# Turning the FFN's activations with transposing DMAs of 16-bit halves, and keeping the tokens stationary in ten of eleven input projections

## The chip, the cores and the metric

The kernel runs on one core of a Trainium2 chip. The metric is device time in microseconds for one execution; the time before is the median of three runs. Engines are named as the profile names them: PE multiplies matrices (PEld is its weight loader, which works beside it), DVE does elementwise vector work, ACT evaluates functions and copies, POOL is the general-purpose engine, and SP issues the DMAs. SBUF is the memory next to the engines (128 partitions); the banks of PSUM receive what PE computes. "Stationary" is the operand that is loaded into PE, "moving" the one that streams through it.

## The reference, cut to what matters

A trunk of two layers over 256 tokens of width 1024, in float32. Each layer is a half-step FFN, a mixer (attention and an mLSTM side by side), and a second half-step FFN, so the kernel computes four FFNs:

```
h = rmsnorm(x, g_pre)                      # 256 x 1024
gate, up = split(h @ w_in, 2)              # w_in: 1024 x 5632
y = (silu(gate) * up) @ w_out              # w_out: 2816 x 1024
x = x + 0.5 * rmsnorm(y, g_post)
```

## The kernel before, in words

**Tiling.** The 256 tokens are two tiles of 128 (`t` = 0, 1). The hidden width of 2816 is cut into eleven chunks of 256 columns, numbered 0 to 10. A chunk needs three weight pieces of 1 MB each: two halves of the input projection (512 rows of `w_in` each, with the chunk's 256 gate and 256 up columns), and one of the output projection (256 rows of `w_out`). The pieces are laid out in DRAM in the order of use, and SP loads them one after another into three buffers (`wr`).

**Float32 from three products.** Each operand is split into a high part in the matmul's 32-bit format and the rest: ACT writes the high part (`wh`, `hh`; line 287 for weights, 545 for activations), DVE the rest (`wl`, `hl`; 288 and 546). A product is high·high + high·rest + rest·high. Weights are split by half pieces (128 x 1024). The split halves live in 7 `wh` and 7 `wl` buffers, and three in ten of them in a further pool of six (`k4`), so about ten halves are held at a time; a `wr` buffer is free for the next load when both its halves have been split.

**Two forms of the input projection.** In chunks 0 and 1 (`TURN = 2`) the tokens are stationary: 128 x 128 blocks of the normalised input are loaded, and 512 weight columns (256 gate, 256 up) stream past. Per chunk that is 2 token tiles x 8 blocks of the width x 3 products = 48 matmuls of 512 columns (`in_piece`, lines 400 to 402). The result has tokens on partitions; ACT takes silu of the gate (line 265, called from 525), DVE multiplies (529), and PE then has to transpose it, 128 x 128 at a time (line 536, four per chunk), because the output projection needs the hidden index on partitions. In chunks 2 to 10 the weights are stationary (`in_turned`): per chunk 4 blocks of 128 hidden columns x 8 blocks of the width, each once with 512 moving columns (both token tiles, high and rest, line 611) and once with 256 (the rest of the weights against the high tokens, line 616), 32 + 32 matmuls. The result comes out already turned, in four banks; ACT and DVE add the two halves of the 512 columns, scale by the token's norm, which now lies along the free dimension (`rows`, made by two PE transposes on line 556), and apply silu and the product (lines 567, 568, 569, 265, 572, two blocks per chunk).

**The output projection** (`out_part`, lines 400 to 402) takes 24 matmuls of 512 columns per chunk, with the turned activations stationary, into four banks that accumulate over the whole FFN. Work is written so that the output projection of a chunk comes after the input projection of the chunk two later (`DEFER = 3`); in the last chunk (10) the remaining three follow.

**What sets the order.** A scheduler orders each engine's instructions when the program is built; every engine then runs its own list strictly in order, and waits at an instruction until its inputs are there. SP's list holds nearly all DMAs, so a DMA that waits there holds those behind it. Only the first chunk of all and the end of each FFN have an order of PE that is written out by hand.

Of the kernel before, what the change touches and what calls it, by code (L numbers as in the profile page):

```python
# [18 lines left out]
F32R = mybir.dt.float32r  # L19
AF = mybir.ActivationFunctionType  # L20
ALU = mybir.AluOpType
# [3 lines left out]
P = 128  # L25
D = 1024
S = 256
NT = S // P
L = 2
DFF = 2816  # L30
NC_FF = DFF // 256
# [5 lines left out]
TURN = 2  # L37
# [93 lines left out]
class _Trunk:  # L131
# [16 lines left out]
    for _n in ("nat", "ra", "rb", "rv", "tmp", "y", "so", "xg"):  # L148
        TAGS[_n] = ("ev", 5)
# [374 lines left out]
    def ffn_hidden(self, pin, r):  # L524
        nc = self.nc
        sil = self.t2("sil", (P, 256))
        self.func(sil, pin[:, 0:256], AF.Silu, scale=r)
        h = self.t2("h", (P, 256))
        nc.vector.scalar_tensor_tensor(h, pin[:, 256:512], r, sil, op0=ALU.mult, op1=ALU.mult)
        return h  # L530

    def ffn_split(self, h):
        nc = self.nc
        ptr = self.bank_tr((P, 2, P))
        for k in range(2):
            nc.tensor.transpose(ptr[:, k, :], h[:, k * P:(k + 1) * P], self.ident)
        hh, hl = self.ffn_operand()
        self.ffn_hilo(ptr, hh, hl)
        return [(hh[:, k, :], hl[:, k, :]) for k in range(2)]
# [7 lines left out]

    def ffn_evac(self, pin, r):
        return self.ffn_split(self.ffn_hidden(pin, r))
# [25 lines left out]
    def ffn_turned(self, banks, rows, late):  # L575


        ops = [self.ffn_operand() for _ in range(2)]
        for j in range(2):
            h = self.ffn_block(banks[j], rows)  # L580
            if late:
                for t in range(NT):
                    self.ffn_hilo(h[:, t], *(v[:, j] for v in ops[t]))
            else:
                self.ffn_hilo(h, *ops[j])
        return [[tuple(v[:, j] for v in ops[t]) if late else tuple(v[:, t] for v in ops[j]) for j in range(2)] for t in range(NT)]

    def ffn(self, pre, gi_post):
# [14 lines left out]
        def in_turned(banks, w, both, last):  # L603


            blocks = [(banks[j][i], slice(i * 256 + j * P, i * 256 + j * P + P)) for j in range(2) for i in range(2)]
            for group, khs in ((blocks, (0,)), (blocks[:2], (1,)), (blocks[2:], (1,))) if last else ((blocks, (0, 1)),):
                for kh in khs:
                    for b, c in group:
                        for k in range(4):  # L610
                            self.nc.tensor.matmul(b, self.cols(w[kh], k)[0][:, c], both[kh][:, k].rearrange("p i t -> p (i t)"),  # L611
                                                  start=kh == 0 and k == 0, stop=False, skip_group_check=True)
                for b, c in group:
                    for kh in khs:
                        for k in range(4):
                            self.nc.tensor.matmul(b[:, 0:NT * P], self.cols(w[kh], k)[1][:, c], both[kh][:, k, 0:NT].rearrange("p i t -> p (i t)"),  # L616
                                                  start=False, stop=kh == 1 and k == 3, skip_group_check=True)

        po, pend = None, []
        if not xT:  # L620
# [12 lines left out]
            h = [self.ffn_evac(pins[t], r[t]) for t in range(NT)]  # L633
            begin = 1
        else:
# [6 lines left out]
            ha = self.ffn_hidden(pa, r[0])  # L642
            yield "second"
            in_piece(0, 0, pa1, w1[0])
            ha = self.ffn_split(ha)
# [6 lines left out]
            hb = self.ffn_evac(pb, r[1])  # L652
            pend = [(0, [ha, hb], self.piece())]
            pb1 = self.bank_pin()
            ha1 = self.ffn_evac(pa1, r[0])
            in_piece(1, 0, pb1, w1[0])
            in_piece(1, 1, pb1, w1[1])
            po = [[self.bank_bk() for _ in range(2)] for _ in range(NT)]
            for t in range(NT):
                out_part(0, t, *pend[0][1:])  # L660
            pend = []
            h = [ha1, self.ffn_evac(pb1, r[1])]
            begin = 2
        for c in range(begin, NC_FF):
# [5 lines left out]
            if c < TURN:  # L670
                pins = [self.bank_pin() for _ in range(NT)]
                for kh in range(2):
                    for t in range(NT):
                        in_piece(t, kh, pins[t], ws[kh])
                h = [self.ffn_evac(pins[t], r[t]) for t in range(NT)]
            else:
                if c == TURN:
                    rows, both = self.token_scales(r), list(self.both)
                banks = [[self.bank_pin() for _ in range(2)], [self.bank_tr() for _ in range(2)]]
                in_turned(banks, ws, both, c == NC_FF - 1)  # L680
                if c == NC_FF - 1:
                    break
                h = self.ffn_turned(banks, rows, c > NC_FF - DEFER - 1)
            if len(pend) == DEFER - 1 or po is None:
                if po is None:
                    po = [[self.bank_bk() for _ in range(2)] for _ in range(NT)]
                cc, hc, wo = pend.pop(0)
                for t in range(NT):
                    out_part(cc, t, hc, wo)

        yield "ending"
        pend.append((c, self.ffn_turned(banks, rows, True), self.piece()))
# [564 lines left out]
```

## Time and profile before

| | |
|---|---|
| median of 3 runs | 974.04 us (973.89 to 974.1) |
| span of the profiled execution | 972.0 us |
| PE busy | 964.9 us, 99% of the span |
| PEld, DVE, ACT busy | 84%, 71%, 58% |
| DMA: bytes, mean rate | 178.94 MB, 184 GB/s |

The profiled execution is shown by its span, from the first to the last instruction; the runs' times also hold what lies around it, some 2 us. Shares are averages over stages of different kinds, so the stage of the FFN that is changed has to be read by itself: a timeline gives the start of every instruction in us from the span's start, how long the group lasts, and, in brackets, how long the engine sat idle before it and for whom. A PE group "x16" is sixteen matmuls in a row, and since they overlap, the cost of one is the distance of starts and not the duration that is listed.

### The profile page before, as it was taken

The numbers are of one execution on the slowest core, as the hardware profiler recorded it, in microseconds if no ns is written. First come the engines' busy times: TensorE is split into PE (matmuls) and PEld (weight loads), VectorE is DVE, ScalarE is ACT, GpSimd is POOL, SyncE is SP. The second block draws the span as 40 slices with busy tenths as digits, with TensorE's granted clock in tenths as the row PEclk, the third lists the DMA queues.
The fourth block names the chain that finished last, engine by engine and source line by source line (L and its number), as shares of the span: only waits on it lengthen the run. The fifth ranks groups of instructions, "written<-read, shape, count | busy, mean of one in ns | idle before, by whom it ended". The sixth has DMA issues, their size and how long they took to land.

```text
span 972.0 us, 13466 instructions
## 1 busy us (share of the span) xinstructions
PE 964.9 (99%) x5067; PEld 818.6 (84%) x5067; DVE 693.2 (71%) x1177; ACT 564.4 (58%) x1041; POOL 30.1 (3%) x55
## 2 busy tenths in 40 slices
PE   9999999999999999999999999999999999999997
PEld 6888888888888888888888888888888888888886
DVE  6786667689867676757687676776998686576764
ACT  7655555577856555555475555455778475645542
POOL 2000000000020000000000000000001000000000
PEclk9999999999999999999999999999999999999999
DMA  8954545336342844554455454543454255555421
GB/s 313 344 185 173 198 187 217 130 130 238 119 185 97 315 168 179 184 206 169 178 212 211 163 214 176 200 190 122 172 205 173 88 206 218 204 182 209 158 102 44
DMA packets 27648, 178.94 MB, mean 184 GB/s; under 512 B 3034, under 2 KB 4186, under 8 KB 6846
## 3 DMA queue, kind: packets, MB, share of 16 engines
q1 hardware_dynamic: 27006, 177.46, 49.5%
q8 instruction: 40, 0.66, 0.3%
q10 hardware_dynamic: 576, 0.61, 0.2%
q14 instruction: 26, 0.21, 0.1%
HBM read 177.01 MB, written 1.05 MB: 183 GB/s over the span
## 4 chain that ended last, share of the span: by engine, by line
PE 99%; DMA 0%; DVE 0%; SPq 0%; ACT 0%; POOLq 0%; issue 0%; DVEq 0%; ACTq 0%
PE pin L611 13%; PE ptr L611 13%; PE bk L400 10%; PE bk L401 10%; PE bk L402 10%; PE pin L400 7%; PE pin L402 7%; PE pin L401 7%; PE ptr L616 7%; PE pin L616 7%; PE ptr L879 1%; PE ptr L426 1%; PE bk L1094 1%; PE bk L1132 1%; DMA x<-in_x_dram 0%; PE bk L378 0%
## 5 line engine op out<-in xcount | busy, mean ns | idle before, releaser
L288 DVE TENSOR_TENSOR wl<-wr,wh 128x1024 fp32r<-128x1024 f32 x324 | 386.0, 1221 | 95.9 <-ACT wh L287 44.8
L287 ACT ACTIVATE wh<-wr 128x1024 fp32r<-128x1024 f32 x324 | 329.1, 1052 | 140.4 <-PE bk L402 38.6
L611 PE MATMUL pin<-both,wh 128*128 128x512 f32 x576 | 142.8, 391 | 0.0
L611 PE MATMUL ptr<-both,wh 128*128 128x512 f32 x576 | 141.5, 390 | 0.0
L400 PE MATMUL bk<-wh,hh 128*128 128x512 f32 x352 | 137.7, 391 | 0.0
L401 PE MATMUL bk<-wl,hh 128*128 128x512 f32 x352 | 137.4, 390 | 0.0
L402 PE MATMUL bk<-wh,hl 128*128 128x512 f32 x352 | 136.2, 389 | 0.0
L611 PEld LDWEIGHTS ptr<-both,wh 128*128 128x128 f32 x576 | 107.3, 188 | 21.9
L611 PEld LDWEIGHTS pin<-both,wh 128*128 128x128 f32 x576 | 107.0, 188 | 21.5
L400 PE MATMUL pin<-wh,both 128*128 128x512 f32 x304 | 122.4, 404 | 0.0
L401 PE MATMUL pin<-wl,both 128*128 128x512 f32 x304 | 119.1, 392 | 0.0
L402 PE MATMUL pin<-wh,both 128*128 128x512 f32 x304 | 118.9, 391 | 0.0
L568 DVE TENSOR_TENSOR su<-pin,su 128x256 f32<-128x256 f32 x72 | 29.3, 421 | 88.1 <-ACT su L567 87.6
L616 PEld LDWEIGHTS pin<-both,wl 128*128 128x128 f32 x576 | 76.0, 191 | 4.1
L402 PEld LDWEIGHTS bk<-wh,hl 128*128 128x128 f32 x352 | 66.1, 188 | 13.9
L616 PE MATMUL pin<-both,wl 128*128 128x256 f32 x576 | 77.7, 283 | 0.0
L545 ACT ACTIVATE hh<-su 128x256 fp32r<-128x256 f32 (+1 forms) x96 | 32.3, 358 | 77.2 <-DVE su L572 47.2
L400 PEld LDWEIGHTS bk<-wh,hh 128*128 128x128 f32 x352 | 66.2, 188 | 12.6
L401 PEld LDWEIGHTS bk<-wl,hh 128*128 128x128 f32 x352 | 66.3, 188 | 12.1
L616 PE MATMUL ptr<-both,wl 128*128 128x256 f32 x576 | 75.8, 283 | 0.0
L616 PEld LDWEIGHTS ptr<-both,wl 128*128 128x128 f32 x576 | 73.1, 192 | 1.3
L402 PEld LDWEIGHTS pin<-wh,both 128*128 128x128 f32 x304 | 57.1, 188 | 12.4
(202 smaller groups left out, 999.8 us busy)
## 6 DMA issues: line engine op xcount, KB each, us to landing
wr<-in_w_dram SPq DMA_DIRECT2D x162, 1024.0 KB, 4.9
gpost<-in_gpost_dram SPq DMA_DIRECT2D x6, 512.0 KB, 5.7
wr<-in_w_dram SPq DMA_DIRECT2D x2, 512.0 KB, 6.4
wr<-in_w_dram SPq DMA_DIRECT2D x3, 256.0 KB, 4.6
x<-in_x_dram SPq DMA_DIRECT2D x3, 256.0 KB, 5.2
out_dram<-x SPq DMA_DIRECT2D x2, 256.0 KB, 2.3
x<-in_x_dram SPq DMA_DIRECT2D x2, 128.0 KB, 2.8
wr<-in_w_dram ACTq DMA_DIRECT2D x1, 256.0 KB, 3.2
```

Source lines behind the costliest of these rows:

```text
L287: ia = nc.scalar.activation(hi, raw[:, j], AF.Copy)
L288: iv = nc.vector.tensor_tensor(lo, raw[:, j], hi.bitcast(F32), op=ALU.subtract)
L400: mm(ps, xh, wh, start=start, stop=False)
L401: mm(ps, xh, wl, start=False, stop=False)
L402: mm(ps, xl, wh, start=False, stop=stop)
L426: nc.tensor.transpose(ptr[:, k, :], x[:, (4 * hf + k) * P:(4 * hf + k + 1) * P], self.ident)
L545: self.nc.scalar.activation(hh, h, AF.Copy)
L568: nc.vector.tensor_tensor(su[:, i], bank[i][:, 0:n], su[:, i], op=ALU.add)
L611: self.nc.tensor.matmul(b, self.cols(w[kh], k)[0][:, c], both[kh][:, k].rearrange("p i t -> p (i t)"), start=kh == 0 and k == 0, stop=Fals ...
L616: self.nc.tensor.matmul(b[:, 0:NT * P], self.cols(w[kh], k)[1][:, c], both[kh][:, k, 0:NT].rearrange("p i t -> p (i t)"), start=False, sto ...
L879: self.T(ptr[:, b, :], a[:, b * P:(b + 1) * P], self.tr.ident)
L1094: self.mm(pcs[c][:, h, :], self.qkT[0][rows, h0 + h, t * P:(t + 1) * P], self.qkT[1][rows, h0 + h, 0:nk], start=True, stop=True)
```

## The change

`TURN` goes from 2 to 10: chunks 0 to 9 now keep the tokens stationary, and only chunk 10 keeps its weights stationary. PE no longer transposes the activations. Instead, per chunk, ACT copies the float32 result of both token tiles (128 x 512) as 1024 16-bit values into two planes, low halves and high halves (`planes`); one transposing DMA on SP's queue turns the eight 128 x 128 blocks of 16-bit values, from SBUF to SBUF (`turned`); and DVE puts the halves together again into float32 (`hT`), which is then split into `hh` and `hl` as before. The result of the input projection goes to the two `pin` banks in odd chunks and to the two `ptr` banks in even ones. The four new tiles share one set of five buffers (`ev`) with tiles of the mixer and the norms. The first output projection of an FFN now comes after chunk 2's input projection instead of chunk 1's.

```diff
@@ -17,6 +17,7 @@
 
 F32 = mybir.dt.float32
 F32R = mybir.dt.float32r
+U16 = mybir.dt.uint16
 AF = mybir.ActivationFunctionType
 ALU = mybir.AluOpType
 AX = mybir.AxisListType
@@ -34,7 +35,7 @@
 EPS = 1e-6
 BIG = -1.0e30
 DEFER = 3
-TURN = 2
+TURN = 10
...
@@ -145,7 +146,7 @@
 
 
     TAGS = {"kwn": ("kwn", 1), "aT0": ("aT0", 1), "aT1": ("aT1", 1)}
-    for _n in ("nat", "ra", "rb", "rv", "tmp", "y", "so", "xg"):
+    for _n in ("nat", "ra", "rb", "rv", "tmp", "y", "so", "xg", "h", "planes", "turned", "hT"):
         TAGS[_n] = ("ev", 5)
 
     def t2(self, nm, shape=(P, 512), dt=F32):
@@ -521,22 +522,26 @@
         region.close()
 
 
-    def ffn_hidden(self, pin, r):
-        nc = self.nc
+    def ffn_hidden(self, pin, r, h):
         sil = self.t2("sil", (P, 256))
         self.func(sil, pin[:, 0:256], AF.Silu, scale=r)
-        h = self.t2("h", (P, 256))
-        nc.vector.scalar_tensor_tensor(h, pin[:, 256:512], r, sil, op0=ALU.mult, op1=ALU.mult)
-        return h
-
-    def ffn_split(self, h):
+        self.nc.vector.scalar_tensor_tensor(h, pin[:, 256:512], r, sil, op0=ALU.mult, op1=ALU.mult)
+
+    def ffn_planes(self, h):
+
+
         nc = self.nc
-        ptr = self.bank_tr((P, 2, P))
-        for k in range(2):
-            nc.tensor.transpose(ptr[:, k, :], h[:, k * P:(k + 1) * P], self.ident)
-        hh, hl = self.ffn_operand()
-        self.ffn_hilo(ptr, hh, hl)
-        return [(hh[:, k, :], hl[:, k, :]) for k in range(2)]
+        planes = self.t2("planes", (P, 2, 512), U16)
+        nc.scalar.activation(planes, h.rearrange("p t j -> p (t j)").bitcast(U16).rearrange("p (n u) -> p u n", u=2), AF.Copy)
+        turned = self.t2("turned", (P, 8, P), U16)
+        nc.sync.dma_start_transpose(turned, planes.rearrange("p u n -> p (u n)"))
+        hT = self.t2("hT", (P, 4, P))
+        nc.vector.tensor_copy(hT.rearrange("p b n -> p (b n)").bitcast(U16).rearrange("p (n u) -> p u n", u=2),
+                              turned.rearrange("p (u b) n -> p u (b n)", u=2))
+        ops = [self.ffn_operand() for _ in range(NT)]
+        for t in range(NT):
+            self.ffn_hilo(hT[:, 2 * t:2 * t + 2], *ops[t])
+        return [[tuple(v[:, k] for v in ops[t]) for k in range(2)] for t in range(NT)]
 
     def ffn_operand(self):
         return [self.hp.tile([P, 2, P], F32R, tag=n, name=self.name(n)) for n in ("hh", "hl")]
@@ -544,9 +549,6 @@
     def ffn_hilo(self, h, hh, hl):
         self.nc.scalar.activation(hh, h, AF.Copy)
         self.nc.vector.tensor_tensor(hl, h, hh.bitcast(F32), op=ALU.subtract)
-
-    def ffn_evac(self, pin, r):
-        return self.ffn_split(self.ffn_hidden(pin, r))
 
     def token_scales(self, r):
 
@@ -572,18 +574,15 @@
         nc.vector.tensor_tensor(su[:, 1], su[:, 1], su[:, 0], op=ALU.mult)
         return su[:, 1].rearrange("p (t j) -> p t j", t=NT)
 
-    def ffn_turned(self, banks, rows, late):
-
-
-        ops = [self.ffn_operand() for _ in range(2)]
+    def ffn_turned(self, banks, rows):
+
+
+        ops = [self.ffn_operand() for _ in range(NT)]
         for j in range(2):
             h = self.ffn_block(banks[j], rows)
-            if late:
-                for t in range(NT):
-                    self.ffn_hilo(h[:, t], *(v[:, j] for v in ops[t]))
-            else:
-                self.ffn_hilo(h, *ops[j])
-        return [[tuple(v[:, j] for v in ops[t]) if late else tuple(v[:, t] for v in ops[j]) for j in range(2)] for t in range(NT)]
+            for t in range(NT):
+                self.ffn_hilo(h[:, t], *(v[:, j] for v in ops[t]))
+        return [[tuple(v[:, j] for v in ops[t]) for j in range(2)] for t in range(NT)]
 
     def ffn(self, pre, gi_post):
         xT, r = pre
@@ -600,11 +599,11 @@
                     self.mm3(po[t][hf], *h[t][k], *self.cols(wo, 2 * k + hf),
                              start=c == 0 and k == 0, stop=c == NC_FF - 1 and k == 1)
 
-        def in_turned(banks, w, both, last):
+        def in_turned(banks, w, both):
 
 
             blocks = [(banks[j][i], slice(i * 256 + j * P, i * 256 + j * P + P)) for j in range(2) for i in range(2)]
-            for group, khs in ((blocks, (0,)), (blocks[:2], (1,)), (blocks[2:], (1,))) if last else ((blocks, (0, 1)),):
+            for group, khs in ((blocks, (0,)), (blocks[:2], (1,)), (blocks[2:], (1,))):
                 for kh in khs:
                     for b, c in group:
                         for k in range(4):
@@ -630,7 +629,10 @@
                 for hf in range(2):
                     self.after(self.square(t, hf, ss), [self.cast])
                 r.append(self.rsqrt_sum(ss, EPS))
-            h = [self.ffn_evac(pins[t], r[t]) for t in range(NT)]
+            h = self.t2("h", (P, NT, 256))
+            for t in range(NT):
+                self.ffn_hidden(pins[t], r[t], h[:, t])
+            h = self.ffn_planes(h)
             begin = 1
         else:
 
@@ -639,27 +641,25 @@
             pa, pa1 = self.bank_pin(), self.bank_pin()
             in_piece(0, 0, pa, w0[0])
             in_piece(0, 1, pa, w0[1])
-            ha = self.ffn_hidden(pa, r[0])
+            h = self.t2("h", (P, NT, 256))
+            self.ffn_hidden(pa, r[0], h[:, 0])
             yield "second"
             in_piece(0, 0, pa1, w1[0])
-            ha = self.ffn_split(ha)
             pb = self.bank_pin()
             in_piece(1, 0, pb, w0[0])
             in_piece(1, 1, pb, w0[1])
             yield "running"
             w1.append(self.piece())
             in_piece(0, 1, pa1, w1[1])
-            hb = self.ffn_evac(pb, r[1])
-            pend = [(0, [ha, hb], self.piece())]
+            self.ffn_hidden(pb, r[1], h[:, 1])
+            pend = [(0, self.ffn_planes(h), self.piece())]
             pb1 = self.bank_pin()
-            ha1 = self.ffn_evac(pa1, r[0])
+            h = self.t2("h", (P, NT, 256))
+            self.ffn_hidden(pa1, r[0], h[:, 0])
             in_piece(1, 0, pb1, w1[0])
             in_piece(1, 1, pb1, w1[1])
-            po = [[self.bank_bk() for _ in range(2)] for _ in range(NT)]
-            for t in range(NT):
-                out_part(0, t, *pend[0][1:])
-            pend = []
-            h = [ha1, self.ffn_evac(pb1, r[1])]
+            self.ffn_hidden(pb1, r[1], h[:, 1])
+            h = self.ffn_planes(h)
             begin = 2
         for c in range(begin, NC_FF):
             ws = [self.piece(), self.piece()]
@@ -668,20 +668,20 @@
                 g = self.load_gpost(gi_post)
                 yield "middle"
             if c < TURN:
-                pins = [self.bank_pin() for _ in range(NT)]
+                pins = [self.bank_pin() if c % 2 else self.bank_tr() for _ in range(NT)]
                 for kh in range(2):
                     for t in range(NT):
                         in_piece(t, kh, pins[t], ws[kh])
-                h = [self.ffn_evac(pins[t], r[t]) for t in range(NT)]
+                h = self.t2("h", (P, NT, 256))
+                for t in range(NT):
+                    self.ffn_hidden(pins[t], r[t], h[:, t])
+                h = self.ffn_planes(h)
             else:
-                if c == TURN:
-                    rows, both = self.token_scales(r), list(self.both)
+                rows, both = self.token_scales(r), list(self.both)
                 banks = [[self.bank_pin() for _ in range(2)], [self.bank_tr() for _ in range(2)]]
-                in_turned(banks, ws, both, c == NC_FF - 1)
-                if c == NC_FF - 1:
-                    break
-                h = self.ffn_turned(banks, rows, c > NC_FF - DEFER - 1)
-            if len(pend) == DEFER - 1 or po is None:
+                in_turned(banks, ws, both)
+                break
+            if len(pend) == DEFER - 1:
                 if po is None:
                     po = [[self.bank_bk() for _ in range(2)] for _ in range(NT)]
                 cc, hc, wo = pend.pop(0)
@@ -689,7 +689,7 @@
                     out_part(cc, t, hc, wo)
 
         yield "ending"
-        pend.append((c, self.ffn_turned(banks, rows, True), self.piece()))
+        pend.append((c, self.ffn_turned(banks, rows), self.piece()))
         for p in pend:
             out_part(p[0], 0, *p[1:])
         yield "done", po[0], g
```

The change moves instructions on every engine. Three places are shown, all in the first FFN around chunks 7 and 8; a name's first number is its running number, which for weights is the piece (20 and 21 are chunk 7's input pieces, 23 and 24 chunk 8's, 26 and 27 chunk 9's, and 25 and 28 the output pieces of chunks 7 and 8).

PE, in the middle of chunk 7's input projection, before (the bank written, then the moving and the stationary operand; `both` holds the tokens' high parts and rests):

```order
L611 MATMUL ptr_114_1244<-both_15_187,wh_21_0_1224 128x512 x2
L611 MATMUL ptr_114_1244<-both_15_187,wh_21_1_1228 128x512 x2
L616 MATMUL pin_111_1241<-both_6_129,wl_20_0_1213 128x256 x2
L616 MATMUL pin_111_1241<-both_6_129,wl_20_1_1217 128x256 x2
L616 MATMUL pin_111_1241<-both_15_187,wl_21_0_1223 128x256 x2
```

and the same projection in the change:

```order
L401 MATMUL pin_119_1119<-wh_21_0_1102,both_15_187 128x512
L402 MATMUL pin_119_1119<-wl_21_0_1101,both_15_187 128x512
L403 MATMUL pin_119_1119<-wh_21_0_1102,both_15_187 128x512
L401 MATMUL pin_119_1119<-wh_21_0_1102,both_15_187 128x512
L402 MATMUL pin_119_1119<-wl_21_0_1101,both_15_187 128x512
```

Weights and tokens have changed sides, and all matmuls are 512 columns wide.

DVE, from the last product of chunk 7's hidden values to that of chunk 8's, in the change (`h` is the product of line 529 before, now line 528; line 289 is the weight split of line 288 before):

```order
L528 SCALAR_TENSOR_TENSOR h_121_1169<-pin_120_1120,rs1_28_283,sil_123_1173 128x256
L289 TENSOR_TENSOR wl_25_1_1240<-wr_25_1234,wh_25_1_1241 128x1024
L289 TENSOR_TENSOR wl_26_0_1341<-wr_26_1339,wh_26_0_1342 128x1024
L539 COPY hT_126_1180<-turned_125_1178 128x2x512
L289 TENSOR_TENSOR wl_26_1_1345<-wr_26_1339,wh_26_1_1346 128x1024
L551 TENSOR_TENSOR hl_128_1183<-hT_126_1180,hh_127_1182 128x256
L551 TENSOR_TENSOR hl_130_1185<-hT_126_1180,hh_129_1184 128x256
L289 TENSOR_TENSOR wl_27_0_1351<-wr_27_1349,wh_27_0_1352 128x1024
L289 TENSOR_TENSOR wl_28_0_1361<-wr_28_1359,wh_28_0_1362 128x1024
L528 SCALAR_TENSOR_TENSOR h_133_1294<-ptr_131_1244,rs1_23_274,sil_134_1295 128x256
L289 TENSOR_TENSOR wl_27_1_1355<-wr_27_1349,wh_27_1_1356 128x1024
L528 SCALAR_TENSOR_TENSOR h_133_1294<-ptr_132_1245,rs1_28_283,sil_135_1298 128x256
```

The copy that puts the halves together waits for the transposing DMA, and behind it on DVE stand four weight splits and the next chunk's product. ACT's list has the same shape: silu, a weight cast, `planes`, two weight casts, then the two casts of `hh`, which wait for that copy.

SP, the DMAs around the transposing DMA of chunk 7, before:

```order
L281 DMA wr_27_1521<-in_w_dram 128x2048
L281 DMA wr_28_1531<-in_w_dram 128x2048
L281 DMA wr_29_1663<-in_w_dram 128x2048
L281 DMA wr_30_1673<-in_w_dram 128x2048
L281 DMA wr_31_1683<-in_w_dram 128x2048
```

and in the change:

```order
L282 DMA wr_26_1339<-in_w_dram 128x2048
L282 DMA wr_27_1349<-in_w_dram 128x2048
L537 DMA_TRANSPOSE turned_125_1178<-planes_124_1176 128x8x128
L282 DMA wr_28_1359<-in_w_dram 128x2048
L282 DMA wr_29_1464<-in_w_dram 128x2048
L282 DMA wr_30_1474<-in_w_dram 128x2048
L537 DMA_TRANSPOSE turned_137_1303<-planes_136_1301 128x8x128
```

Every third weight load now has a transposing DMA ahead of it, which waits on ACT's `planes`; that of chunk 7 stands behind the loads of chunk 9's input pieces and ahead of the output piece 28.

## The prediction

> **What bounds the kernel now.** I read the page's busy times first, then its chain of waits, then busy time by window and the wait lists of SP and ACT.
>
> ```profile
> span 972.0 us, 13466 instructions
> PE 964.9 (99%) x5067; PEld 818.6 (84%) x5067; DVE 693.2 (71%) x1177; ACT 564.4 (58%) x1041; POOL 30.1 (3%) x55
> ...
> PE 99%; DMA 0%; DVE 0%; SPq 0%; ACT 0%; POOLq 0%; issue 0%; DVEq 0%; ACTq 0%
> ...
> 19.30:330.00 310.70, 310.70 (x1639) 262.88 (x1639) 233.58 (x396) 192.68 (x360) 11.23 (x17) 1.00 0.52 190
> 800.00:972.00 172.00, 165.70 (x869) 142.46 (x867) 109.20 (x185) 82.35 (x145) 1.10 (x2) 0.99 0.44 162
> ...
> SPq L281 <- DVE wl L288: 604.3, 97, 15.1
> ...
> ACT wh L287 <- PE bk L402: 38.6, 16, 4.4
> ```
>
> PE is the whole chain. In the window rows the first pair is length and PE's busy time: from 19.3 to 330 us PE has no gap, and the 7 us that it idles in all lie at the ends (6.3 of them after 800). Everything else is throttled by PE: SP waits 604 us for the split that frees a load buffer, and ACT waits for PE to free a half. So the time falls only if PE's list gets shorter, and rises only if something makes PE wait. The clock column is 1.00 throughout; no term rests on it.
>
> **PE's list.** The FFN's steady chunk, in PE's timeline (start, length, group), fourth FFN, chunk after chunk:
>
> ```profile
> 871.84 3.11 PE L611 MATMUL pin<-both,wh 128*128 128x512 f32 x13
> ...
> 879.09 2.08 PE L616 MATMUL pin<-both,wl 128*128 128x256 f32 x16
> ...
> 882.92 0.40 PE L400 MATMUL bk<-wh,hh 128*128 128x512 f32 x1
> ...
> 888.39 1.98 PE L611 MATMUL pin<-both,wh 128*128 128x512 f32 x8
> ...
> 957.38 0.39 PE L400 MATMUL bk<-wh,hh 128*128 128x512 f32 x1
> ...
> 964.86 0.39 PE L400 MATMUL bk<-wh,hh 128*128 128x512 f32 x1
> ```
>
> The 32 matmuls of 512 columns take 879.09 − 871.84 = 7.25 us (227 ns each), the 32 of 256 take 882.92 − 879.09 = 3.83 us (120 ns, where half of 227 would be 113), the output projection 5.47 us; the chunk's period is 16.55 us. A pure run of 512-column matmuls with tokens or activations stationary is the last pair: 33 matmuls in 7.48 us, 226.7 ns. The columns are equal on both sides (32·768 = 48·512), so the change saves only what the short matmuls cost beyond their columns, and the slower start that follows them. A chunk becomes 48 + 24 = 72 matmuls, 72 · 0.2267 = 16.32 us: 0.23 us less, in 8 chunks of 4 FFNs: **−7.4 us**. Bounds: the slowest rows of such a run are those behind PE's transposes (next fence: five matmuls from 25.47 to 26.63, 232 ns each); if the input part ran so throughout, it would take 11.14 us instead of 11.08 and the term would be +1.9. −7.4 is also the lower end, and the nearest row, since no transposes are left there.
>
> The Trainium skill's "TensorE: Matmul & The Clock Gate", section "Back-to-back issue gap", puts a matmul at columns / 2.4 + 2.5 ns, 215.8 and 109.2 ns here; by it a chunk would gain 32·(215.8 + 109.2) − 48·215.8 = 42 ns and the term would be −1.3 us. The rows are 11 ns above it at both widths, which weighs double for the short ones, and the rows decide.
>
> Chunks 0 and 1 lose PE's transposes:
>
> ```profile
> 21.84 0.39 PE L400 MATMUL pin<-wh,both 128*128 128x512 f32 x1
> ...
> 24.79 0.38 PE L536 MATMUL ptr<-c,h 128*128 128x128 f32 x2
> ...
> 25.47 0.39 PE L400 MATMUL pin<-wh,both 128*128 128x512 f32 x1
> ...
> 26.63 0.39 PE L402 MATMUL pin<-wh,both 128*128 128x512 f32 x1
> ...
> 27.54 0.39 PE L536 MATMUL ptr<-c,h 128*128 128x128 f32 x2
> ...
> 30.08 0.39 PE L402 MATMUL pin<-wh,both 128*128 128x512 f32 x1
> ...
> L536 PE MATMUL ptr<-c,h 128*128 128x128 f32 x32 | 6.1, 271 | 0.0
> ```
>
> From 21.84 to 30.08 there are 34 starts of 512-column matmuls to go, 34 · 0.2267 = 7.71 us, and 8.24 us pass: 0.26 us per pair of transposes. With 32 transposes in all, 16 pairs: **−4.2 us** (between −3 and −5, since the slowdown behind a pair is of unequal length). The transposes for `rows` stay. Sum: −11.6 us, if the new route is hidden.
>
> **The new route: what it costs on ACT and DVE.**
>
> ```profile
> L288 DVE TENSOR_TENSOR wl<-wr,wh 128x1024 fp32r<-128x1024 f32 x324 | 386.0, 1221 | 95.9 <-ACT wh L287 44.8 <-PE ptr L616 25.8 <-PE ptr L611 13.0
> L287 ACT ACTIVATE wh<-wr 128x1024 fp32r<-128x1024 f32 x324 | 329.1, 1052 | 140.4 <-PE bk L402 38.6 <-DMA wr<-in_w_dram 36.4 <-PE ptr L611 30.6
> L546 DVE TENSOR_TENSOR hl<-su,hh 128x256 fp32r<-128x256 f32 x48 | 20.1, 422 | 9.5 <-ACT hh L545 8.9
> L545 ACT ACTIVATE hh<-su 128x256 fp32r<-128x256 f32 x48 | 19.7, 414 | 45.6 <-DVE su L572 31.1 <-PE bk L401 14.4
> L529 DVE SCALAR_TENSOR_TENSOR h<-pin,rs,sil 128x256 f32<-128x256 f32 x14 | 6.6, 478 | 0.0
> L265 ACT ACTIVATE sil<-pin,rs 128x256 f32<-128x256 f32 x14 | 6.4, 468 | 7.0 <-POOL rs L415 3.8 <-PE pin L402 3.1
> L265 ACT ACTIVATE qk<-conv 128x1024 f32<-128x1024 f32 x2 | 2.1, 1064 | 0.6 <-DVE conv L910 0.6
> L569 DVE TENSOR_TENSOR su<-su,rows 128x256 f32<-128x256 f32 x144 | 56.9, 419 | 0.6
> ```
>
> `planes` is 1024 values a partition on ACT: between 0.47 (256 values) and 2.1 (double the 1024-value rows); I take 1.06. DVE's copy is 1024 values: between 0.42 and 2.4, taken at 1.22. ACT then works 6·1.052 + 2·0.468 + 1.06 + 2·0.414 = 9.1 us per chunk, DVE 6·1.221 + 2·0.478 + 1.22 + 2·0.422 = 10.3 us; the ten su operations that go (some 0.42 each) made DVE's before 12.4. Both stay below 16.3, so they cost nothing while PE covers them.
>
> **The transposing DMA.** No row shows one. Call T the time from the end of `planes` to the landing.
>
> ```profile
> wr<-in_w_dram SPq DMA_DIRECT2D x162, 1024.0 KB, 4.9
> ...
> out_dram<-x SPq DMA_DIRECT2D x2, 256.0 KB, 2.3
> ...
> lamv<-in_lam_dram SPq DMA_DIRECT2D x1, 256.0 KB, 8.9
> ...
> out_dram<-x SPq DMA_DIRECT2D x2, 128.0 KB, 2.2
> ...
> 113.84:121.10 7.26, 7.26 (x34) 1.00 0.66 223
> 121.10:124.93 3.83, 3.83 (x34) 1.00 0.95 366
> 124.93:130.40 5.47, 5.47 (x27) 1.00 0.06 25
> ```
>
> 256 KB out of SBUF land in 2.3 us with nothing ahead (the lower end); 8.9 is a 256 KB load in finely cut pieces among others; if its eight 128 x 128 blocks were worked off one after the other like eight small DMAs, 8 · 2.2 = 17.6 is the upper end. One weight load ahead adds up to 4.9, but the DMA is issued as an output projection begins, and there the queue is nearly empty (share 0.06, the column before the last). I take 5 us: 2.3, and about half a load ahead of it.
>
> What waits for it: not PE directly. Chunk c's activations are used after two input and two output projections more (2·10.9 + 2·5.4 = 32.6 us). But DVE's copy waits, with weight splits behind it, and ACT's `hh` behind the copy. Along the order shown, one turn from `planes` to the next `planes` is T + copy 1.22 + split 1.22 + two `hl` 0.84 + two splits 2.44 + product 0.48 + split 1.22 + product 0.48 + `planes` 1.06 = T + 8.96. Up to T = 16.32 − 8.96 = 7.4 us PE sets the pace. At 5 the turn is 14.0, 2.3 us spare, which also holds a copy or `planes` of double price (one of them; with both, T may be 5.1). The price in PE time is then 0. On SP, the load behind the DMA waits for `planes` too, but its buffer comes free with the split ahead of the copy, about the time at which `planes` ends, so it loses little; it has until after `hh`. The 40 transposes move 10.5 MB beside 179.
>
> Above 7.4 a lead is used up first: chunk c+2's first half is split T + 4.5 us after chunk c's projection ends (silu, product, `planes` 2.1, T, copy, split) and needed after 5.4 + 10.9 + 5.4 = 21.8. With nine turns an FFN loses 9(T − 7.4) − (17.3 − T) = 10T − 83.9 us: nothing up to T = 8.4, then 40 us in the kernel per us of T.
>
> The Trainium skill speaks against the change: "VectorE: DVE Perf Modes", section "The three transpose paths", gives 1309 ns for a 128x128 transpose by DMA against 390 ns on TensorE. Eight of 1309 in series would be T = 10.5, an estimate from that page, and 84 us lost by the formula. "DMA: Bandwidth & Descriptors", section "Latency and other measured facts", gives 261 GB/s, 1.0 us for 256 KB, by which T stays near the 2.3 us row. No run so far tells them apart.
>
> **The rivals.**
> A, forecast: T below 8.4. Span 972.0 − 11.6 = 960.4; the median of the runs lies 974.04 − 972.0 = 2.0 above the span, so 962.4. Own range 961 to 966.
> B, slower: the eight blocks go largely in series; T = 10, the middle of 2.3 and 17.6. The loss is 4 · 16.1 = 64 us: 962.4 + 64 = 1027; at T = 17.6 it would be 962.4 + 368 = 1331. It decides against the change from T = 8.7 (10T − 83.9 = 2.9). For it: eight separate blocks, and nothing in the trace that moves 16-bit values. Against it: 256 KB is a quarter of a weight load, and the queue is idle at that moment.
> C, half the gain: the input part runs at 230 ns, between the two runs above (48 · 0.230 = 11.04, a term of −1.3), or PE waits some us at an FFN's start. There the first FFN is tightest: chunk 2 now comes 5.47 us earlier, and on DVE its second piece stands behind the first copy. Gain 4 to 6: 968 to 970 (−1.3 − 4.2 gives 968.5). Against it: 7.25 / 32 = 227 ns with the DMA queue at 0.66, the same as at 0.06, so traffic does not slow PE.
> D, no change: T close to 8.7, or losses at the FFN's starts that just eat the gain. 972 to 976.
>
> A 0.60, C 0.14, D 0.06, B 0.20. A and C are faster by more than 0.2% (2 us), which is about what a measurement of this kernel tells from none; so are, of D, few: faster 0.72, same 0.08, slower 0.20. The range takes A, C, D and the mildest of B: 960 to 985.
>
> **What would show it.** Right: PE starts 227 ns apart and 16.3 us from chunk to chunk in all four FFNs, no L536 row, SP's transposing DMA landing within 8 us, DVE idle before the copy (2 to 3 us a chunk) without PE idle. Wrong: PE idle for `wh` or `wl` in the late chunks of an FFN, growing from chunk to chunk (B), or only in the first three (C); a turn of `planes` longer than 16.3 us; or stationary tokens at 230 ns and more.

## The result and the profile after

The changed kernel takes 962.5 us (962.02 to 962.97) against 974.01 us, a ratio of 0.9882 [0.9868, 0.9896]. Its profiled span is 960.2 us where that of before was 972.0.

From its page, the busy times and the chain of waits by engine:

```profile
span 960.2 us, 12037 instructions
PE 952.8 (99%) x4523; PEld 788.9 (82%) x4523; DVE 638.7 (67%) x945; ACT 571.2 (59%) x937; POOL 29.5 (3%) x55
...
PE 97%; DVE 1%; DMA 1%; ACT 0%; issue 0%; POOLq 0%; DVEq 0%; ACTq 0%
```

PE still is the chain. Its busy time fell by 12.1 us (964.9 − 952.8), the span by 11.8 (the sum of the prediction was 11.6): the gain is a shorter list on PE, and next to nothing of it was given back as idle time. By windows (length, then busy time of PE, PEld, DVE, ACT, POOL with counts, granted clock, DMA share, GB/s), the same two stretches as before, and the two parts of one steady chunk:

```profile
19.30:330.00 310.70, 310.62 (x1512) 257.63 (x1512) 221.87 (x339) 197.20 (x337) 10.69 (x17) 1.00 0.60 201
800.00:960.20 160.20, 153.62 (x694) 127.43 (x692) 90.32 (x123) 78.69 (x112) 1.10 (x2) 0.99 0.53 176
110.93:121.81 10.88, 10.88 (x49) 9.01 (x48) 6.81 (x9) 5.58 (x8) 0.00 (x0) 1.00 0.53 194
121.81:127.25 5.44, 5.44 (x25) 4.50 (x24) 2.55 (x3) 3.08 (x4) 0.00 (x0) 1.00 0.61 196
```

From 19.3 to 330 us PE is busy all but 0.08 us, at full clock. PE's timeline (start, length, group) shows where the parts of that chunk begin:

```profile
110.93 0.39 PE L401 MATMUL pin<-wh,both 128*128 128x512 f32 x1
111.16 0.39 PE L402 MATMUL pin<-wl,both 128*128 128x512 f32 x1
...
121.81 0.39 PE L401 MATMUL bk<-wh,hh 128*128 128x512 f32 x1
...
127.25 0.39 PE L401 MATMUL ptr<-wh,both 128*128 128x512 f32 x1
```

The 48 matmuls of the input part take 10.88 us, 226.7 ns each, the 24 of the output part 5.44: a period of 16.32 us, where it was 16.55. By PE's timeline each of the four FFNs has six periods of 16.32 us in a row and one of 16.45 or 16.46 behind them. The matmuls run at that spacing although the tokens now are the stationary side.

The groups of the new route (busy us, mean ns, idle time before them), and the transposing DMA beside a weight load (KB, median us from issue to landing):

```profile
L289 DVE TENSOR_TENSOR wl<-wr,wh 128x1024 fp32r<-128x1024 f32 x324 | 389.2, 1221 | 180.4 <-ACT wh L288 174.4
...
L535 ACT ACTIVATE planes<-h 128x1024 uint16<-128x1024 uint16 x40 | 42.1, 1052 | 8.6 <-DVE h L528 8.4
...
L539 DVE COPY hT<-turned 128x1024 uint16<-128x1024 uint16 x40 | 30.3, 757 | 41.9 <-DMA turned<-planes 41.5
...
wr<-in_w_dram SPq DMA_DIRECT2D x162, 1024.0 KB, 5.2
...
turned<-planes SPq DMA_TRANSPOSE x40, 4.4
```

and the line that issues it on SP, where the last row gives the spread from issue to landing:

```profile
L537 SPq DMA_TRANSPOSE turned<-planes x40: 1237/1238/3697, 23.6 to 923.0; - x40
...
DMA to landing us min/median/max: 2.7/4.4/8.9
```

From the end of `planes` to the start of DVE's copy it is 4.5 us on the mean of the 40 (2.8 to 9.3). The prediction's T ends with the landing; the two agree where the copy waits for the DMA, which it does 27 times of 40, and elsewhere DVE is still busy, so that the landing was earlier. DVE waits 41.5 us for it in the whole kernel, one us a chunk, and ACT's `hh` waits for DVE:

```profile
ACT hh L550 <- DVE hT L539: 46.0, 31, 4.3
...
SPq L282 <- DVE wl L289: 464.6, 88, 15.6
...
SPq L537 <- ACT planes L535: 76.0, 31, 9.3
...
PE bk L390 <- PEq L1247: 0.8, 1, 0.8
```

The last row is the one wait that the list has of PE; the others are of engines that have room. SP still waits 465 us for the splits that free load buffers (604 before), so the 1.24 us that it takes to issue a transposing DMA are hidden too.

### The profile page after: what moved, and what is told of

It is laid out like the page before. It is cut to its first block, busy times and chain, and to the rows that moved or that the text cites. A ratio compares the mean times of both kernels' runs of the same rounds, so it can differ in the third digit from the quotient of the medians.

```text
span 960.2 us, 12037 instructions
## 1 busy us (share of the span) xinstructions
PE 952.8 (99%) x4523; PEld 788.9 (82%) x4523; DVE 638.7 (67%) x945; ACT 571.2 (59%) x937; POOL 29.5 (3%) x55
## 3 DMA queue, kind: packets, MB, share of 16 engines
HBM read 177.01 MB, written 1.05 MB: 185 GB/s over the span
## 4 chain that ended last, share of the span: by engine, by line
PE 97%; DVE 1%; DMA 1%; ACT 0%; issue 0%; POOLq 0%; DVEq 0%; ACTq 0%
PE pin L401 13%; PE pin L402 13%; PE pin L403 13%; PE bk L401 10%; PE bk L402 10%; PE bk L403 10%; PE ptr L402 6%; PE ptr L403 6%; PE ptr L401 6%; PE pin L610 1%; PE ptr L610 1%; PE ptr L879 1%; PE ptr L427 1%; DMA wr<-in_w_dram 1%; PE bk L1094 1%; PE ptr L615 1%
## 5 line engine op out<-in xcount | busy, mean ns | idle before, releaser
L289 DVE TENSOR_TENSOR wl<-wr,wh 128x1024 fp32r<-128x1024 f32 x324 | 389.2, 1221 | 180.4 <-ACT wh L288 174.4
L401 PE MATMUL pin<-wh,both 128*128 128x512 f32 x560 | 221.2, 396 | 0.0
L403 PE MATMUL pin<-wh,both 128*128 128x512 f32 x560 | 218.3, 390 | 0.0
L402 PE MATMUL pin<-wl,both 128*128 128x512 f32 x560 | 218.2, 390 | 0.0
L403 PEld LDWEIGHTS pin<-wh,both 128*128 128x128 f32 x560 | 105.1, 188 | 22.3
L401 PEld LDWEIGHTS pin<-wh,both 128*128 128x128 f32 x560 | 105.3, 188 | 22.0 <-issue 0.7
L402 PEld LDWEIGHTS pin<-wl,both 128*128 128x128 f32 x560 | 105.3, 188 | 20.6
L403 PE MATMUL ptr<-wh,both 128*128 128x512 f32 x256 | 99.4, 389 | 0.0
L402 PE MATMUL ptr<-wl,both 128*128 128x512 f32 x256 | 99.4, 389 | 0.0
L401 PE MATMUL ptr<-wh,both 128*128 128x512 f32 x256 | 98.9, 389 | 0.0
L539 DVE COPY hT<-turned 128x1024 uint16<-128x1024 uint16 x40 | 30.3, 757 | 41.9 <-DMA turned<-planes 41.5
L401 PEld LDWEIGHTS ptr<-wh,both 128*128 128x128 f32 x256 | 48.1, 188 | 10.0
L402 PEld LDWEIGHTS ptr<-wl,both 128*128 128x128 f32 x256 | 48.1, 188 | 10.0
L550 ACT ACTIVATE hh<-hT 128x256 fp32r<-128x256 f32 x80 | 28.9, 409 | 46.0 <-DVE hT L539 46.0
L403 PEld LDWEIGHTS ptr<-wh,both 128*128 128x128 f32 x256 | 48.1, 188 | 9.9
```

Of the source, the lines that this page charges most:

```text
L289: iv = nc.vector.tensor_tensor(lo, raw[:, j], hi.bitcast(F32), op=ALU.subtract)
L401: mm(ps, xh, wh, start=start, stop=False)
L402: mm(ps, xh, wl, start=False, stop=False)
L403: mm(ps, xl, wh, start=False, stop=stop)
L539: nc.vector.tensor_copy(hT.rearrange("p b n -> p (b n)").bitcast(U16).rearrange("p (n u) -> p u n", u=2), turned.rearrange("p (u b) n -> p ...
L550: self.nc.scalar.activation(hh, h, AF.Copy)
```

## The experiments

There are twelve runs, each group beside the kernel before on the same chip (its medians there: 973.69, 973.72, 973.77 and 973.79 us); two of them repeat a kernel. From here on T is the mean time from the end of `planes` to the start of DVE's copy over the 40 pairs of a run's timelines.

### PE's transposes kept, weights moving in all ten chunks (pe_turn10)

```diff
 (kernel before)
-TURN = 2
+TURN = 10
```

> The kernel before with tokens stationary in chunks 0 to 9, but still turned by PE's transposes: no transposing DMA. Theory A (the gain is PE's shorter list): the short matmuls go (-7.4 us), 64 more pairs of transposes at 0.26 us come (+16.6): 974.0 + 9.2 = 983.2 us. Rival E (short matmuls cost hardly more than their columns, -1.3 us): 989.3. Rival F (the gain is DVE's relief from the su operations, which this kernel has too): below 974.

Measured: 982.93 us, 1.0095 [1.0081, 1.0109]. Its page:

```profile
span 981.5 us, 12234 instructions
...
L536 PE MATMUL ptr<-c,h 128*128 128x128 f32 x160 | 30.4, 271 | 0.0
```

There are 128 more transposes than before, 64 pairs. The terms of the prediction make −7.4 + 64 · 0.26 = +9.2 us; the medians differ by 9.2. So the first half of the change without the second is a loss: the transposes cost PE more than the short matmuls do, and it is the DMA that lets the 7.4 us be had. DVE's relief from the `su` operations, which this kernel has too, is not the gain.

### The transposing DMA in chunks 0 and 1 alone (dma_two)

```diff
 (changed kernel)
-TURN = 10
+TURN = 2
 (from chunk 2 on the turned projection of the kernel before)
```

> The change with the weights stationary again from chunk 2 on: only chunks 0 and 1 are turned by DMA, the first output projection still behind chunk 2's input. Theory A: only the transposes' term is left, 974.0 - 4.2 = 969.8 us (968.5 to 971). Rival F (DVE's relief): 973 to 974, since DVE keeps its su operations in eight chunks. Rival C (PE waits at the FFN's start, where the first output projection was moved): 971 to 974.

Measured: 969.05 us, 0.9953 [0.9940, 0.9965].

```profile
span 967.4 us, 13398 instructions
PE 959.9 (99%) x5035; PEld 815.1 (84%) x5035; DVE 696.9 (72%) x1185; ACT 572.1 (59%) x1049; POOL 32.9 (3%) x55
```

The transposes of two chunks are worth 972.0 − 967.4 = 4.6 us (4.2 forecast), the eight other chunks the rest, 967.4 − 960.2 = 7.2 us (7.4 forecast).

### The new projection without its route (no_turn)

```diff
 (changed kernel, ffn_planes)
-        (planes, the transposing DMA and the copy into hT)
+        hT = h.rearrange("p t (k n) -> p (t k) n", k=2)
```

The activations enter the output projection unturned, so this kernel computes something else; PE's list is that of the change.

> The change without turning at all: planes, transposing DMA and the copy are left out, and the activations enter the output projection unturned, so that the output is another; PE's list is the same. Theory A (the whole route is hidden behind PE): 962.5 us, within 1. Rival G (the sum agreed because a missed gain paid for a missed cost of the route): 955 to 960.

Measured: 961.49 us, 0.9878 [0.9865, 0.9892], span 959.5. What `planes`, the DMA and the copy cost beside PE is thus 0.7 us of span, 1.0 between the medians: they are hidden but for that, as the sum took them.

### Each transposing DMA twice (chain2)

```diff
 (changed kernel, ffn_planes)
-        nc.sync.dma_start_transpose(turned, ...)
+        for _ in range(2):
+            nc.sync.dma_start_transpose(turned, ...)
```

> The change with each transposing DMA issued twice in a row into the same tile, so that T goes from 4.4 us (issue to landing in the profile) to about 8; the scheduler sees both. Theory A: one turn is T + 8.5 with the measured copy of 0.76, so 16.5 against PE's 16.3, and the lead takes the rest: 962.5 to 965 us. Rival H (SP's order matters too: the load behind the DMAs is held for the second wait, and PE runs out of weights): 970 or more.

Measured: 964.89 us, 0.9911 [0.9891, 0.9932], span 962.5. T rose to 8.8 us. The waits for the copy and of PE:

```profile
DVE hT L540 <- DMA turned<-planes: 123.5, 37, 7.0
...
PE ptr L401 <- DVE h L528: 1.9, 1, 1.9
```

DVE's wait trebled (41.5 to 123.5 us), and PE waited 1.9 us. So 4 us more of T cost 2.3 us of span. But the scheduler that orders the instructions knew of the second DMA and put the copy later among the weight splits, so this does not price T in a fixed order. The next runs hold the copy's place there.

### One to seven transposing DMAs with the copy's place held (pin1, pin2, pin3, pin4, pin7)

```diff
 (changed kernel; from chunk 4 on the copy and the casts of hh keep their places among the weight splits)
+            if c > 3:
+                cast, copy = self.held[-2]
+                self.turns = [[], [(None, copy)], [(cast, None)]]
...
+        for _ in range(N):    # N = 1, 2, 3, 4, 7
             nc.sync.dma_start_transpose(turned, ...)
```

First one, four and seven were run.

> The change with the place of the copy and of the casts behind it on DVE and ACT held where the scheduler had put them in chunks 2 to 8 (behind the first half of the piece two chunks later), as a base for the next two. Theory A and the rivals alike: 962.5 us, within 2.

> The same held order with each transposing DMA issued four times in a row: T of about 4.4 + 3 x 2.75 = 12.7. On ACT one turn is then T + copy 0.76 + two hh 0.83 + three casts 3.16 + planes 1.05 = T + 5.8 = 18.5 against 16.3: theory A loses 2.2 us a turn in seven held turns of an FFN, less a lead of some 7: 4 x 8 = 33, so 995 us (970 to 1015), with PE waiting in the later chunks. Rival J (a late transpose never reaches PE, since 32 us lie between the two projections): 965.

> The same with seven in a row: T about 4.4 + 6 x 2.75 = 21, the turn 26.7, 10.4 us over. Theory A: 8 turns x 10.4 less a lead near 0, 83 us an FFN, 4 x 83: 1290 us (1200 to 1330); the step from four to seven is some 35 us of kernel per us of T. Rival J: 965 to 990.

Measured: 961.74 us (0.9877 [0.9863, 0.9892]), 1204.45 us (1.2370 [1.2339, 1.2401]) and 1541.04 us (1.5835 [1.5806, 1.5863]). With one DMA, holding the place costs nothing; the two others missed their numbers by 209 and 251 us, in the direction of the theory. A part of that was T itself, which had not been read but assumed. With four in a row, SP's and DVE's timelines of one turn:

```profile
152.64 1.23 SPq L539 DMA_TRANSPOSE turned<-planes  x1
155.96 0.33 SPq L283 DMA_DIRECT2D wr<-in_w_dram  x1
158.19 1.23 SPq L539 DMA_TRANSPOSE turned<-planes  x1
159.51 0.55 SPq L283 DMA_DIRECT2D wr<-in_w_dram  x1
163.72 4.61 SPq L539 DMA_TRANSPOSE turned<-planes  x2
...
169.85 0.74 DVE L541 COPY hT<-turned 128x1024 uint16<-128x1024 uint16 x1 [10.36 <-DMA turned<-planes]
170.48 0.86 DVE L529 SCALAR_TENSOR_TENSOR h<-pin,rs,sil 128x256 f32<-128x256 f32 x2
...
189.83 0.75 DVE L541 COPY hT<-turned 128x1024 uint16<-128x1024 uint16 x1 [4.64 <-DMA turned<-planes]
```

The first three stand among weight loads, 5.5 us apart, and T is 17.2 in this turn. A repeat writes the same tile, so SP issues it only when the one before it has landed: its waits for that come to 306.5 us, 123 times, in this run. Means: 4.7 us with one, 16.7 with four, 25.3 with seven; a repeat cost 4.0 us up to the fourth and 2.9 beyond. Set against T as measured, the spans (960.4, 1199.1, 1538.0) gave a new theory: (1538.0 − 1199.1) / (25.3 − 16.7) = 39.4 us per us of T, which leads back to no loss at 10.6 us. Two and three in a row were run to test it.

> The order of copy and casts is held as in the run with one transposing DMA a chunk; here two stand in a row. T is read as the mean time from the end of planes to the start of DVE's copy: 4.7 us with one, 16.7 with four, 25.3 with seven, where the spans are 960.4, 1199.1 and 1538.0. Theory K (nothing is lost up to a threshold, then a fixed price): the last two give (1538.0 - 1199.1) / (25.3 - 16.7) = 39.4 us per us of T and a threshold of 16.7 - (1199.1 - 960.4) / 39.4 = 10.6 us. With two, T should be about 8.8 (as with two in the free order), below it: 961.5 to 965 us. Rival L (no threshold, every us of T costs): the line through one and four, 19.9 us per us, gives 960.4 + 4.1 x 19.9 = 1042 for the span, 1044 us. Rival M (the threshold as the prediction worked it out, 8.4, and 40 us per us): 960.4 + 0.4 x 40 = 976 for the span, 978 us.

> The same held order with three transposing DMAs in a row. T should be about 12.7 us, halfway between two (8.8) and four (16.7). Theory K (threshold 10.6, 39.4 us per us): 960.4 + 2.1 x 39.4 = 1043 for the span, 1045 us; if T is 11.7 or 13.7, 1003 or 1082 for the span. Rival L (no threshold, 19.9 us per us): 960.4 + 8.0 x 19.9 = 1120 for the span, 1122 us. Rival M (threshold 8.4, 40 us per us): 960.4 + 4.3 x 40 = 1132 for the span, 1134 us. Whatever T turns out, the pair of T and span has to lie on the one line or the other. Under K PE's waits should be for hh and the products h, as with four, and of some 2 us a chunk.

Measured: 994.76 us (1.0231 [1.0183, 1.0278]) and 1089.91 us (1.1170 [1.1122, 1.1218]).

| in a row | T, us | span, us | over one | 39.4 · (T − 10.6) | the prediction's 40T − 336 |
|---|---|---|---|---|---|
| 1 | 4.7 | 960.4 | 0 | 0 | 0 |
| 2 | 9.1 | 994.6 | 34 | 0 | 28 |
| 3 | 14.0 | 1092.3 | 132 | 134 | 224 |
| 4 | 16.7 | 1199.1 | 239 | (fitted) | 332 |
| 7 | 25.3 | 1538.0 | 578 | (fitted) | 676 |
| 2, free order | 8.8 | 962.5 | 2 | 0 | 16 |

With three, the new line holds to 2 us (the profiled execution is the longest of four, which spread from 1084.16 to 1094.09 us), and the two rivals (185 by the line without a threshold, 9.3 · 19.9, and 224) fall. With two it fails by 34 us, and there the prediction's formula is near, with 28. No single line fits all the rows. PE's waits, first with three, then with two:

```profile
PE bk L402 <- ACT hh L553: 69.0, 20, 11.2
PE ptr L562 <- DVE h L529: 7.3, 4, 2.4
PE pin L402 <- ACT hh L553: 7.2, 2, 4.2
PE pin L402 <- ACT wh L289: 5.8, 2, 4.5
```

```profile
PE bk L402 <- ACT hh L553: 7.5, 3, 4.7
PE pin L614 <- DVE h L529: 6.6, 6, 2.5
PE ptr L403 <- DVE wl L290: 2.8, 4, 1.6
```

PE waits most for the activations `hh` and the products `h`, and less for the weights `wh` and `wl`, for which the prediction had it wait. With two, T is not one value: it runs from 5.5 to 17.9 us, and nine of the 40 turns lie above 10.6, by 19.5 us in all. Of the 34 us, 14.3 are PE's busy time (967.1 us beside 952.8) and 19.9 its idle time. That the nine late turns make the idle time is not shown: with two in the free order five turns lie above 10.6, by 18.1 us, and 2 us were lost.

The rows of the table differ in more than T. What is held is the copy's place among the weight splits; where the next chunk's product `h` stands was left to the scheduler. With one, three or four splits stand between the copy and that product in most turns, as in the changed kernel; in DVE's timeline of pin1 four of them lie between these two lines:

```profile
111.75 0.76 DVE L540 COPY hT<-turned 128x1024 uint16<-128x1024 uint16 x1 [2.59 <-DMA turned<-planes]
...
120.73 0.48 DVE L529 SCALAR_TENSOR_TENSOR h<-pin,rs,sil 128x256 f32<-128x256 f32 x1
```

With three, four and seven the product comes right behind the copy in nearly all turns (169.85 and 170.48 above), and with two both occur. So the three largest rows nearly share an order and give the slope, but the order of the smallest is another, and the 10.6 us are not a threshold of one order.

The same T of about 9 costs 34 us here and 2 us in the free order. DVE's timelines show a difference in some of the turns. Held order, two in a row:

```profile
130.50 0.75 DVE L541 COPY hT<-turned 128x1024 uint16<-128x1024 uint16 x1 [8.39 <-DMA turned<-planes]
131.14 0.47 DVE L529 SCALAR_TENSOR_TENSOR h<-pin,rs,sil 128x256 f32<-128x256 f32 x1
131.53 3.49 DVE L290 TENSOR_TENSOR wl<-wr,wh 128x1024 fp32r<-128x1024 f32 x3
134.93 0.48 DVE L529 SCALAR_TENSOR_TENSOR h<-pin,rs,sil 128x256 f32<-128x256 f32 x1
```

Free order, two in a row:

```profile
113.31 2.36 DVE L289 TENSOR_TENSOR wl<-wr,wh 128x1024 fp32r<-128x1024 f32 x2 [2.00 <-ACT wh L288]
116.90 0.76 DVE L540 COPY hT<-turned 128x1024 uint16<-128x1024 uint16 x1 [1.22 <-DMA turned<-planes]
...
123.03 0.48 DVE L528 SCALAR_TENSOR_TENSOR h<-pin,rs,sil 128x256 f32<-128x256 f32 x1
```

Held, DVE idles 8.39 us and the next chunk's product `h` comes right behind the copy, and the bank that it reads comes free only then. Free, two splits stand ahead of the copy, DVE idles 1.22 us, and the product comes 6 us later. In the first chunks of each FFN the free order too has the product right behind the copy, and that the place of the copy or of the product makes the difference was not run by itself.

### Chunk 10 by DMA too (all_dma)

```diff
 (changed kernel, last chunk; abridged)
-                rows, both = self.token_scales(r), list(self.both)
...
-                in_turned(banks, ws, both)
+                pins, h = [self.bank_tr() for _ in range(NT)], []
+                for t in range(NT):
+                    for kh in range(2):
+                        in_piece(t, kh, pins[t], ws[kh])
+                    ht = self.t2("h", (P, NT, 256))[:, 0:1]
+                    self.ffn_hidden(pins[t], r[t], ht[:, 0])
+                    h += self.ffn_planes(ht, 1)
                 break
```

Each token tile of the last chunk is turned as soon as it is there, with one transposing DMA for each plane.

> The change carried on to chunk 10: there too the tokens are stationary and the transposing DMA turns the activations, each token tile by itself (the first tile's projection is done ahead of the second's), and the two PE transposes of the token scales go with it. Theory A: per FFN 32 short matmuls (11.08 - 48 x 0.2267 = 0.2 us) and one pair of transposes (0.26) less, 1.8 us in the kernel, if the first tile's activations (wanted 10.9 us after its projection: 5.4 of the second's, 5.4 of two output parts) arrive in time: T 4.4 + 5 = 9.4. So 960 to 961.5 us beside 962.5. Rival I (the end of an FFN is tight: the route of the last chunk is exposed, or its casts hold ACT ahead of the next stage): 965 or more.

Measured: 959.2 us, 0.9855 [0.9838, 0.9871]. Since that interval touches the one of the change, both were run again in the same rounds.

> The changed kernel once more, beside the version whose last chunk is turned by DMAs too, on one chip and in the same rounds, to tell the two apart: their intervals against the kernel before (0.9868 to 0.9896 and 0.9838 to 0.9871) touch. Theory A (the last chunk's short matmuls and transposes are PE time like those of the others): 961.5 to 963 us here.

> The version whose last chunk is turned by DMAs too, in the same rounds as the changed kernel. Theory A: the 2.8 us by which its profiled span is shorter (957.4 against 960.2) stand in the times too: 2.5 to 3.5 us below the changed kernel, 958.5 to 960.5 us. Rival: the difference seen so far is between two sets of rounds, and the two kernels lie within 1 us.

Measured: 962.40 us (962.16 to 962.60) and 959.48 us (959.22 to 959.73), 2.9 us apart. The page of the first run of this version:

```profile
span 957.4 us, 11870 instructions
PE 949.8 (99%) x4451; PEld 784.8 (82%) x4451; DVE 631.5 (66%) x913; ACT 570.0 (60%) x917; POOL 30.0 (3%) x55
...
turned<-planes SPq DMA_TRANSPOSE x56, 3.6
```

PE's list is 72 instructions and 3.0 us shorter than that of the change (952.8), about what the span fell by (2.8): 16 more transposing DMAs are hidden like the 40. The gain is more than the 1.8 us that were expected, and 959.2 lies below the expected 960 to 961.5; what the other 1.2 us on PE are stays open. This version beats both kernels.

## Why the prediction was right

**PE's list, −7.4 and −4.2: right, each by itself.** The period is 16.32 us as worked out, and the two halves measured 7.2 and 4.6 us, so the sum is off by 0.2 us because two misses of opposite sign nearly cancel. pe_turn10 checked the two terms once more, with the transposes of the other sign. The Trainium skill's "TensorE: Matmul & The Clock Gate", section "Back-to-back issue gap", gives the gap of isolated matmuls, which would have made the first term −1.3 us; the rows decided, rightly. The lesson is in the 7 ns by which the 256-column matmul (120 ns) is above half of the 512-column one (113): 32 times a chunk, 32 chunks.

**The route's costs: right, with the copy too dear.** `planes` 1.05 us (1.06 taken). The copy 0.76 (1.22 taken): its row has 1024 16-bit values, and it was priced by rows of f32 values. T 4.5 us (5 taken). That 5 came so near is in part luck: no row backed it within 2.3 to 17.6, and the forecast needed only a T below 8.4. DVE's idle time before the copy was to be 2 to 3 us a chunk and is 1.0; most of its idle time lies before the weight splits, which wait for ACT's casts (180 us in the row of L289). Hardly any of it reaches PE (no_turn: 0.7 us).

**B, the blocks in series: wrong premise.** A transposing DMA lands in 2.7 us at the least, beside 2.1 us for a plain 256 KB out of SBUF in the same run:

```profile
out_dram<-x SPq DMA_DIRECT2D x2, 256.0 KB, 2.1
```

Eight blocks cost little more than one plain transfer of the same size. Eight times the 1309 ns of the Trainium skill's "VectorE: DVE Perf Modes", section "The three transpose paths", was 10.5 us: the runs show that this figure is not a price per block. The same section says that the crossbar path reaches about 90% of the DMA bandwidth, which the prediction left out. No run here measures that rate, but 2.7 beside 2.1 us lies nearer to it than to a price per block.

**C and D: not seen.** The tokens stationary run at 226.7 ns, not 230, and no FFN's start costs PE a wait (its list of waits has that one row of 0.8 us, which was there before).

**The price of a late T: the slope fits, the threshold stays open.** The prediction's 40 us per us of T is 39.4 between four and seven DMAs. Its formula, whose loss begins at 8.4, gives 28 us with two, where 34 were lost, and 224 with three, where 132 were. The turn in it, "T + 8.96", was added up along the order of the changed kernel. With four, `planes` to `planes` is 21.6 us on the mean of four turns at a mean T of 17.2, that is T + 4.4: the products come right behind the copy there, and splits, casts and `hl` are done while the next T runs. What PE's waits are put down to then is `hh` (144.8 us) and `h` (20.4), and no weight split; 40.3 of the 144.8 stand at an input projection, which does not read `hh`, so what is waited for there stays open. No run keeps the changed kernel's own order at a mean T above 7.4, so T + 8.96 was not tested, and what a late T would have cost this kernel as it stands is open. Rival B's 1027 us at T = 10 was not run either. Since T came out at 4.5, none of this touched the forecast.

**Two slips.** The clock column was called 1.00 throughout, and its second row has 0.99; no term rests on it. The chances of A and C add up to 0.74, which "faster" at 0.72 falls short of.

**In the expectations**, T was mis-sized: a repeat was put at 2.75 us, about the shortest landing (2.7), and it cost 4.0, since it waits for the landing of the one before it and stands among weight loads.

## What to carry to other kernels

Where PE is the chain, count matmuls by their spacing and not by their columns: short ones and transposes between them cost more than their share here, and a route over other engines that stays off PE's chain costs next to nothing (0.7 us of span here, at T = 4.5 and a period of 16.32). Price such a turn by what actually stands between its waits in program order, and read its longest transfer from the trace before pricing it. Half of this change alone (weights moving, PE still transposing) loses 9 us, so its parts should be judged together.

## What was not expected of the hardware

- Transposing DMAs of 256 KB move in small packets: on their queue there are 42240 more of them than before for 10.49 MB more, some 248 bytes each and 1056 to a DMA (the rows give packets and MB, first before, then after). Weight loads beside them landed in 5.2 us instead of 4.9.

```profile
q1 hardware_dynamic: 27006, 177.46, 49.5%
q1 hardware_dynamic: 69246, 187.95, 58.0%
```

- PE slows down where it is made to wait: with four DMAs in a row, PE's busy time for the same 4523 matmuls rose from 952.8 to 1026.5 us, and the granted clock (third column from the end) fell to 0.91 in the second FFN. In PE's timeline of that run a wait of 3.90 us (to 150.47) is followed by matmuls that start some 0.43 us apart for nearly 3 us, and 0.23 us apart after that. The group of matmuls that waits for `hh` took 463 ns each on the mean, instead of 390:

```profile
383.00:622.00 239.00, 199.99 (x830) 162.45 (x829) 114.15 (x151) 101.69 (x148) 2.16 (x4) 0.91 0.68 192
...
L402 PE MATMUL bk<-wh,hh 128*128 128x512 f32 x352 | 163.0, 463 | 104.5 <-ACT hh L553 104.5
```

  The Trainium skill's "TensorE: Matmul & The Clock Gate", section "HAM oscillation — how this bites in real kernels", warns of idle gaps above some 3.4 us; the longest waits here are 12 us, and the clock column agrees.
- SP needs 1.24 us to issue one transposing DMA, where a weight load takes it 0.33 us in the same timeline.
